# Seven products of quarters for six of eight c and h tiles and for the gates of a gated-convolution decoder step, with a second read of its input

## The chip, the cores and the metric

The kernel runs on one core of one Trainium2 chip. The metric is the device time of one execution in microseconds (us), lower is better. "The time" of a kernel is the median of its runs; the profile comes from one more execution.

## The reference, cut to what matters

The program is one layer of a decoder for 576 tokens (512 of a prompt, 64 of samples) of 1024 channels, all in float32. In this document's names:

```python
xn = rms_norm(h, g_mix)
z = xn @ w_in                         # 1024 x 6144: b, c, hc, v, gate a, gate b
ya = b * conv_w3(c * hc) @ w_out_conv
yb = pool(v) @ w_pool * pool_scale    # trailing means minus the token, by groups
h = h + (sigmoid(a) * ya + sigmoid(bg) * yb) @ w_o
h = h + square(relu(rms_norm(h, g_mlp) @ w_up)) @ w_down
h = h + sigmoid(rms_norm(h, g_ple) @ w_ple_gate) * (p @ w_ple_proj)
y = rms_norm(h, g_final)
```

The last rows of the convolution's and the pooling's inputs are outputs too.

## The kernel before, in words

Channels lie on the partitions, in 8 tiles of 128; the tokens lie in two halves of 288 columns. Every operand is split into a rounded part and the rest (`hi` and `lo`, lines 82 to 94: one cast on ScalarE, one subtraction on VectorE), and every product is three matmuls: hi x hi, hi x lo, lo x hi. A product of one output tile (`product`, line 113) is 8 k x 3 x 2 halves = 48 matmuls of 288 columns. Weights are streamed: `Stream` (line 175) takes a list `order` of parts (128 x 512), loads them on SP's queue into eight raw buffers and splits them into seven pairs of buffers (NF = 7), so that up to six split parts lie ahead of the one in use and loads up to six parts ahead of the splits. A part of a plain tile feeds 24 matmuls.

The mixer comes first. Tile 0 of c, h and b is computed as the input arrives (line 358 on, `psf`). Then, for tiles 1 to 7, a loop computes c, h and b (line 372 on): c is scaled by the squared norm (`r1s`, L375), u = c times h (L381, L384), the three taps are one ScalarE and two VectorE operations (L391, L393), b is scaled (L398), multiplied with the convolution (L400, L403) and split as an operand. Eight gate tiles (L415, L417), eight tiles of `w_oc` (L421), and four groups of pooling with their gates (L432 to L483) follow. At this point the scratch and PSUM pools are closed and others opened (line 489 on), w_o is applied and added to the input, which has stayed in `xall` (L609).

The MLP's first product (w_up) is already done with seven products of quarters for each pair of output tiles q and q+4 (`pairs_of`, line 539). The two output tiles, the two halves of the tokens and the two halves of the 1024 inputs make a 2 x 2 by 2 x 2 block product. `Operand` (line 511) holds, for each of four k, split blocks b11, b22, b21 and four differences of blocks t1 to t4. `Form` (line 152) makes weight blocks a, b, d, two sums made by an accumulating DMA on POOL's queue (s1 = c+d, s0 = c+a, L149) and two made on VectorE (s2, L169; s3, L171). One `quarter` (line 495) is 4 k x 3 = 12 matmuls of 288 columns into one PSUM bank; seven per pair, and VectorE combines them with five operations of 288 columns (L564 to L568, L593, L595), after one ScalarE copy (L544). The first MLP block enters late, with the last k of four quarters moved back. Here the matmuls are kept in program order by hand. Elsewhere a scheduler orders each engine's queue ahead of time, by readiness in its model and by place in the program; on the chip each queue runs in order.

After the MLP come w_ple_proj and w_ple_gate (`psg`), and the final norm.

Of the kernel before, what the change touches and what calls it, by code (L numbers as in the profile page):

```python
# [7 lines left out]
F32 = mybir.dt.float32  # L8
# [4 lines left out]
P = 128  # L13
D = 1024
NJ = D // P
# [27 lines left out]
def tile_hybrid_step(ctx: ExitStack, tc: tile.TileContext, x, pt, vecs, rc, ident, sconv, spool, w_first, w_in,  # L43
# [12 lines left out]
    tmp = scope.enter_context(tc.tile_pool(name="tmpx", bufs=8))  # L56
    psum = scope.enter_context(tc.tile_pool(name="psumx", bufs=4, space=bass.MemoryType.PSUM))
    banks = None

    def matmul(*args, **kw):  # L60

        i = nc.tensor.matmul(*args, **kw)  # L62
        if banks is not None:
            tc.keep_in_program_order(i)
# [158 lines left out]
    for b in range(NFB):  # L223
        pairs = [Pair(w_up[b * NJ + q], w_up[b * NJ + NQ + q]) for q in range(NQ)]
        order += [Form(pairs[0], "a")]
        for q in range(NQ):
            order += [Form(pairs[q], n) for n in ("s2", "s0", "s1", "b")]
            if q + 1 < NQ:
                order += [Form(pairs[q + 1], "a")]
            order += [Form(pairs[q], n) for n in ("d", "s3")]  # L230
        for j in range(NJ):
            order += unit(w_down[b * NJ + j])
# [13 lines left out]
    xall = const.tile([P, NJ, NH, HT], F32, tag="xall", name="xall")  # L246
    xs = [xall[:, j] for j in range(NJ)]
# [44 lines left out]
    sp = tmp.tile([P, NJ, DB, PB], F32, tag="sp", name="sp", bufs=1)  # L292
    nc.sync.dma_start(sp, spool)


    class Rms:
# [48 lines left out]
        def copies(self, r, tag, square=None):  # L345
            out = const.tile(self.shape, F32, tag=tag, name=tag)
# [5 lines left out]
            return out, out2  # L352


    stat = Rms()
    for j in range(NJ):
        stat.add(xs[j], part=j >= NJ - 2)
    ps0 = [psum.tile([P, NH, 512], F32, tag="ps", name="psf") for _ in range(3)]
# [8 lines left out]
    ncp_t = tmp.tile([P, NJ, CW - 1], F32, tag="ncp", name="ncp_t", bufs=1)  # L367
    npp_t = tmp.tile([P, NJ, PB], F32, tag="npp", name="npp_t", bufs=1)


    ya_in = []
    for j in range(NJ):
        ps_c = ps0[0] if j == 0 else product(stream.take(2), xg)
        c = tmp.tile([P, NH, HT], F32, tag="t", name="c")
        nc.vector.tensor_tensor(out=c, in0=halves(ps_c), in1=r1s, op=ALU.mult)  # L375
        ps_h = ps0[1] if j == 0 else product(stream.take(2), xg)
        u = tmp.tile([P, CEXT], F32, tag="ext", bufs=4, name="u")
        us = u[:, CE:].rearrange("p (b t) -> p b t", b=DB)
        nc.gpsimd.memset(u[:, :CW - 1], 0.0)
        nc.gpsimd.tensor_copy(us[:, :, :CW - 1], sc[:, j])  # L380
        nc.vector.tensor_tensor(  # L381
            out=u[:, CW - 1:CE].rearrange("p (h t) -> p h t", h=NH),
            in0=prompt(ps_h), in1=prompt(c), op=ALU.mult)
        nc.vector.tensor_tensor(  # L384
            out=us[:, :, CW - 1:].rearrange("p (h b) t -> p h b t", h=NH),
            in0=sample(ps_h), in1=sample(c), op=ALU.mult)
        nc.gpsimd.tensor_copy(ncp_t[:, j], u[:, CE - (CW - 1):CE])
        nc.gpsimd.tensor_copy(sc[:, j], us[:, :, DS:])
        n = CEXT - (CW - 1)
        cv = tmp.tile([P, CEXT], F32, tag="ext", bufs=4, name="cv")  # L390
        nc.scalar.mul(cv[:, :n], u[:, :n], v(W_CONV, j))  # L391
        for k in range(1, CW):
            nc.vector.scalar_tensor_tensor(  # L393
                out=cv[:, :n], in0=u[:, k:k + n], scalar=v(W_CONV + k, j), in1=cv[:, :n],
                op0=ALU.mult, op1=ALU.add)
        ps_b = ps0[2] if j == 0 else product(stream.take(2), xg)
        bt = tmp.tile([P, NH, HT], F32, tag="t", name="bt")
        nc.vector.tensor_tensor(out=bt, in0=halves(ps_b), in1=r1, op=ALU.mult)  # L398
        ya = tmp.tile([P, NH, HT], F32, tag="t", name="ya")
        nc.vector.tensor_tensor(  # L400
            out=prompt(ya), in0=prompt(bt), in1=cv[:, :SEQ].rearrange("p (h t) -> p h t", h=NH),
            op=ALU.mult)
        nc.vector.tensor_tensor(  # L403
            out=sample(ya), in0=sample(bt),
            in1=cv[:, CE:].rearrange("p (b t) -> p b t", b=DB)[:, :, :DS].rearrange(
                "p (h b) t -> p h b t", h=NH),
            op=ALU.mult)
        ya_in.append(split_act(ya))


    mix = []
    for j in range(NJ):
        ps = product(stream.take(2), xg)
        z = tmp.tile([P, NH, HT], F32, tag="t", name="z")
        nc.vector.tensor_tensor(out=z, in0=halves(ps), in1=r1, op=ALU.mult)  # L415
        g = keep.tile([P, NH, HT], F32, tag="keep", name="ga")
        nc.scalar.activation(g, z, AF.Sigmoid)  # L417
        mix.append(g)
# [66 lines left out]
    for o, t in ((ncp, ncp_t), (ncs, sc), (npp, npp_t), (nps, sp)):  # L485
        nc.sync.dma_start(o, t)
# [3 lines left out]
    tmp = scope.enter_context(tc.tile_pool(name="tmpm", bufs=3))  # L490
    psum = scope.enter_context(tc.tile_pool(name="psumm", bufs=1, space=bass.MemoryType.PSUM))
    banks = scope.enter_context(tc.tile_pool(name="banks", bufs=6, space=bass.MemoryType.PSUM))
    acts2 = scope.enter_context(tc.tile_pool(name="acts2", bufs=6))

    def quarter(o, w, bs, ks, start, stop):
        for k in ks:
            wh, wl = (t[:, k * P:(k + 1) * P] for t in w)
            hi, lo = bs[k]
            for i, (wt, at) in enumerate(((wh, hi), (wh, lo), (wl, hi))):
                matmul(o, wt, at, start=start and k == 0 and i == 0,  # L500
                       stop=stop and k == NQ - 1 and i == 2, skip_group_check=True)

    def two_products(operands, ks):

        two = [(w, [bank() for _ in range(NH)]) for w in (stream.take(2), stream.take(2, live=2))]
        for part in (ks[:-2], ks[-2:]):
            for w, ps in two:
                steps(ps, w, operands, part, first=ks[0], last=ks[-1])
        return [ps for _, ps in two]

    class Operand:

        def __init__(self):
            self.f = {n: [None] * NQ for n in ("b11", "b22", "b21", "t1", "t3", "t2", "t4")}
            self.shared = None

        def two(self, k, src, names):
            parts = split(src, [P, NH, HT], acts2 if k == 0 else acts, "act")
            for i, n in enumerate(names):
                self.f[n][k] = tuple(t[:, i] for t in parts)  # L520

        def add(self, k, g):

            if k % 2 == 0:
                self.shared = tuple(acts.tile([P, NH, HT], F32R, tag="act", name=n) for n in ("hi", "lo"))
            self.two(k, g[:, 1:3], ("b11", "b22"))
            hi, lo = (t[:, k % 2] for t in self.shared)
            nc.scalar.copy(hi, g[:, 3])
            nc.vector.tensor_tensor(out=lo, in0=g[:, 3], in1=as32(hi), op=ALU.subtract)
            self.f["b21"][k] = hi, lo  # L530
            t = tmp.tile([P, 4, HT], F32, tag="g", name="gt", bufs=2)
            nc.vector.tensor_tensor(  # L532
                out=t[:, 0:2], in0=g[:, 0:1].broadcast_to([P, 2, HT]), in1=g[:, 1:3], op=ALU.subtract)
            nc.vector.tensor_tensor(out=t[:, 2], in0=g[:, 2], in1=t[:, 0], op=ALU.subtract)  # L534
            nc.vector.tensor_tensor(out=t[:, 3], in0=g[:, 3], in1=t[:, 2], op=ALU.subtract)
            self.two(k, t[:, 0:2], ("t1", "t3"))
            self.two(k, t[:, 2:4], ("t2", "t4"))

    def pairs_of(n, op, corner, finish, late=False, between=None):


        def copied(pa):
            g = tmp.tile([P, 4, HT], F32, tag="g", name="g", bufs=2)
            nc.scalar.copy(g[:, 1], pa)  # L544
            return g

        def begin(w):
            pa = bank()
            quarter(pa, w, op.f["b11"], range(NQ), True, True)
            return pa, copied(pa)  # L550
# [264 lines left out]
```

## Time and profile before

| | us |
|---|---|
| median of 3 runs | 907.16 (905.72 to 907.32) |
| the profiled execution, its own time | 907.29 |
| its span, first to last instruction | 905.5 |
| TensorE busy | 890.5 |
| VectorE busy | 520.6 |
| ScalarE busy | 374.4 |
| GpSimd busy | 111.2 |

PE is TensorE's matmuls, PEld its weight loads, DVE VectorE, ACT ScalarE, POOL GpSimd, SP the queue that issues most DMAs. A letter q behind an engine means its instruction queue. L89 is line 89 of the kernel. The profiled execution's time is 1.8 us longer than its span.

### The profile page before, as it was taken

Reading aid. Unit: us, or ns where it says so; the run is one execution under the profiler, and the core shown is the slowest. Engines: PE = TensorE matmul, PEld = TensorE weight load, DVE = VectorE, ACT = ScalarE, POOL = GpSimd, SP = SyncE. Lnnn points to the kernel's source line nnn. Section 1 sums busy time; section 2 is a strip of 40 time slices with the busy share of each in tenths; the row PEclk is TensorE's granted clock in tenths of the full one; section 3 lists DMA queues with packets and bytes.
Section 4 is the critical chain, followed back from the end, with each engine's and each line's share of the span. In section 5 each row is a group of like instructions: output and inputs, shape, how many; then the busy total and the mean of one; then the engine's idle time right before and its main releaser. Section 6 shows DMA issues by size and latency. Waiting matters only on the chain.

```text
span 905.5 us, 16619 instructions
## 1 busy us (share of the span) xinstructions
PE 890.5 (98%) x6674; PEld 887.7 (98%) x6674; DVE 520.6 (57%) x880; ACT 374.4 (41%) x642; POOL 111.2 (12%) x148
## 2 busy tenths in 40 slices
PE   9999999999999999999999999999999999999995
PEld 8999999999999999999999999999999999999995
DVE  7554544433335767857884337633773467687455
ACT  8332222322112333344675337622673157546432
POOL 3000000000002210112110100010100110021354
PEclk9999999999999999999999999999999999999998
DMA  7422222222222222334453545444544444332002
GB/s 256 156 82 84 82 83 82 85 83 82 82 83 85 81 82 86 112 83 95 118 160 99 140 106 140 128 112 110 137 133 105 111 125 134 97 96 93 24 10 96
DMA packets 52654, 93.66 MB, mean 103 GB/s; under 512 B 6241, under 2 KB 9953, under 8 KB 52577
## 3 DMA queue, kind: packets, MB, share of 16 engines
q1 hardware_dynamic: 47824, 84.18, 29.5%
q0 software_dynamic: 4608, 8.39, 5.9%
q8 instruction: 52, 0.85, 0.4%
q14 instruction: 26, 0.20, 0.1%
q10 hardware_dynamic: 144, 0.03, 0.0%
HBM read 89.60 MB, written 2.99 MB: 102 GB/s over the span
## 4 chain that ended last, share of the span: by engine, by line
PE 93%; DVE 3%; ACT 1%; issue 1%; DMA 1%; SPq 0%; DVEq 0%; ACTq 0%
PE b L62 46%; PE ps L62 39%; PE psg L62 6%; PE psf L62 2%; DVE lo L89 1%; PE psn L322 1%; PE psn L340 1%; DMA raw<-w_up 1%; DMA xall<-x 1%; DVE xall L609 0%; ACT hi L88 0%; DVE gt L534 0%; DVE gt L532 0%; DVE xall L697 0%; ACT sq L307 0%
## 5 line engine op out<-in xcount | busy, mean ns | idle before, releaser
L88 ACT CAST hi<-raw 128x512 fp32r<-128x512 f32 x290 | 178.5, 621 | 384.4 <-PE ps L62 205.6
L89 DVE TENSOR_TENSOR lo<-raw,hi 128x512 fp32r<-128x512 f32 x290 | 204.4, 709 | 145.8 <-ACT hi L88 140.9
L62 PE MATMUL b<-hi 128*128 128x288 f32 x1120 | 276.4, 296 | 2.7 <-ACT hi L88 1.3
L62 PE MATMUL b<-lo,hi 128*128 128x288 f32 x1120 | 275.9, 295 | 0.1
L62 PE MATMUL b<-hi,lo 128*128 128x288 f32 x1120 | 275.9, 295 | 0.0
L62 PEld LDWEIGHTS b<-hi 128*128 128x128 f32 x1120 | 192.3, 188 | 3.7 <-ACT hi L88 1.7
L62 PEld LDWEIGHTS b<-lo,hi 128*128 128x128 f32 x1120 | 192.3, 188 | 0.3 <-DVE lo L89 0.3
L62 PEld LDWEIGHTS b<-hi,lo 128*128 128x128 f32 x1120 | 192.3, 188 | 0.0
L62 PE MATMUL ps<-lo,hi 128*128 128x288 f32 x880 | 188.5, 296 | 0.0
L62 PE MATMUL ps<-hi 128*128 128x288 f32 x880 | 188.5, 296 | 0.0
L62 PE MATMUL ps<-hi,lo 128*128 128x288 f32 x880 | 188.3, 296 | 0.0
L62 PEld LDWEIGHTS ps<-hi 128*128 128x128 f32 x880 | 141.9, 189 | 0.0
L62 PEld LDWEIGHTS ps<-lo,hi 128*128 128x128 f32 x880 | 141.9, 189 | 0.0
L62 PEld LDWEIGHTS ps<-hi,lo 128*128 128x128 f32 x880 | 141.9, 189 | 0.0
L149 POOL DMA_DIRECT2D raw<-w_up x32 | 27.9, 872 | 326.4 <-DMA raw<-w_up 186.1
L313 POOL TENSOR_TENSOR sq<-sq 128x576 f32<-128x576 f32 (+2 forms) x32 | 41.1, 1284 | 113.1 <-ACT sq L307 63.8
L62 PE MATMUL psg<-hi 128*128 128x320 f32 (+1 forms) x128 | 38.1, 298 | 0.7 <-ACT r L347 0.7
L62 PE MATMUL psg<-lo,hi 128*128 128x320 f32 (+1 forms) x128 | 37.9, 296 | 0.0
L62 PE MATMUL psg<-hi,lo 128*128 128x320 f32 (+1 forms) x128 | 37.9, 296 | 0.0
L89 DVE TENSOR_TENSOR lo<-s,hi 128x512 fp32r<-128x512 f32 x32 | 22.0, 691 | 15.8 <-ACT hi L88 15.1
L89 DVE TENSOR_TENSOR lo<-g,hi 128x576 fp32r<-128x576 f32 x32 | 26.4, 834 | 6.6 <-ACT hi L88 6.6
L307 ACT ACTIVATE sq<-xall 128x576 f32<-128x576 f32 (+2 forms) x39 | 22.5, 585 | 18.1 <-DVE xall L726 18.1
(124 smaller groups left out, 704.0 us busy)
## 6 DMA issues: line engine op xcount, KB each, us to landing
raw<-w_in SPq DMA_DIRECT2D x90, 256.0 KB, 2.7
raw<-w_up SPq DMA_DIRECT2D x80, 256.0 KB, 2.9
raw<-w_down SPq DMA_DIRECT2D x64, 256.0 KB, 2.9
raw<-w_up POOLq DMA_DIRECT2D x32, 256.0 KB, 4.3
raw<-w_oc SPq DMA_DIRECT2D x16, 256.0 KB, 2.7
raw<-w_o SPq DMA_DIRECT2D x16, 256.0 KB, 2.7
raw<-w_pg SPq DMA_DIRECT2D x16, 256.0 KB, 2.8
xall<-x SPq DMA_DIRECT2D x7, 288.0 KB, 5.3
```

Source lines behind the costliest of these rows:

```text
L62: i = nc.tensor.matmul(*args, **kw)
L88: nc.scalar.copy(hi, src)
L89: nc.vector.tensor_tensor(out=lo, in0=src, in1=as32(hi), op=ALU.subtract)
L149: nc.gpsimd.dma_start(raw, y, accum_op=ALU.add)
L307: i = nc.scalar.activation(sq, t, AF.Square)
L313: nc.gpsimd.tensor_tensor(out=self.parts[0], in0=self.parts[0], in1=sq, op=ALU.add)
L322: nc.tensor.matmul(sums[:, i:i + 1], a[:, h, c:c + m], ones32[:, 0:1], start=k == 0, stop=k == len(self.parts) - 1)
L340: nc.tensor.matmul(self.ps[:, h, c:c + m], self.y[:, i:i + 1].broadcast_to([m, P]), idt[:m, :m], start=True, stop=True)
```

## The change

Tiles 1 to 3 and 5 to 7 of c and of h, and all eight gate tiles, are computed in pairs (q, q+4) by the seven products of quarters; tiles 0 and 4 of c and h, and all tiles of b, stay plain. In a block of one q the pair of c comes first, then the pair of h with b of tile q in between (`filler`), then b of tile q+4. The operand is the scaled input `xg`, whose split tiles serve as b11, b22 and b21 as they are; only the differences are made, in the iterations of tiles 0 and 4, in part in ten buffers of their own. The matmuls of these parts are kept in program order. The convolution becomes a class with parts by half. The mixer's scratch has four buffers of a tile instead of eight; pools are opened so that a new tile waits for the old tiles under it alone (`reuse_waits="tile"`), and one set of pools more is used (gates and pooling are now in different ones). The input lies in the eight `keep` buffers, which the gates take over, and is loaded a second time into `xall` when the pooling ends. The pooling state is loaded, and the convolution state stored, between the gates and `w_oc`. Helpers moved up unchanged are left out here.

```diff
-    tmp = scope.enter_context(tc.tile_pool(name="tmpx", bufs=8))
-    psum = scope.enter_context(tc.tile_pool(name="psumx", bufs=4, space=bass.MemoryType.PSUM))
+    def pool(name, bufs, **kw):
+        return scope.enter_context(tc.tile_pool(name=name, bufs=bufs, reuse_waits="tile", **kw))
+    tmp, acts2 = pool("tmpx", 4), pool("acts1", 10)
+    psum = pool("psumx", 1, space=bass.MemoryType.PSUM)
+    banks = pool("banksx", 6, space=bass.MemoryType.PSUM)
...
-    for j in range(1, NJ):
-        order += unit(w_in[NJ + j]) + unit(w_in[2 * NJ + j]) + unit(w_in[j])
-    for j in range(NJ):
-        order += unit(w_in[4 * NJ + j])
+    order += unit(w_in[NJ + NQ]) + unit(w_in[2 * NJ + NQ]) + unit(w_in[NQ])
...
+    for q in range(1, NQ):
+        order += forms([Pair(w_in[i * NJ + q], w_in[i * NJ + NQ + q]) for i in (1, 2)],
+                       unit(w_in[q]), unit(w_in[NQ + q]))
+    order += forms([Pair(w_in[4 * NJ + q], w_in[4 * NJ + NQ + q]) for q in range(NQ)])
...
-    xall = const.tile([P, NJ, NH, HT], F32, tag="xall", name="xall")
-    xs = [xall[:, j] for j in range(NJ)]
+    xs = [keep.tile([P, NH, HT], F32, tag="keep", name="xin") for _ in range(NJ)]
...
+    ya_in = [None] * NJ
+    for j in (0, NQ):
...
+        conv.gate(ps0[2] if j == 0 else product(stream.take(2), xg))
+        for k in range(j // 2, j // 2 + 2):
+            g = tmp.tile([P, 4, HT], F32, tag="g", name="gx", bufs=2)
+            for i in range(2):
+                nc.scalar.mul(g[:, 2 * i:2 * i + 2], xs[k + i * NQ], v(G_MIX, k + i * NQ))
+            xo.differences(k, g)
+    pinned = True
+    for q in range(1, NQ):
+        def corner(i, g, c11):
+            if i == 0:
+                conv.lo = tmp.tile([P, NH, HT], F32, tag="t", name="c")
+                nc.vector.tensor_tensor(out=conv.lo[:, 1], in0=c11, in1=r1s[:, 1], op=ALU.mult)
+            else:
+                conv.now.half(1, c11, conv.lo[:, 1])
+        def finish(i, g):
+            if i == 0:
+                nc.vector.tensor_tensor(out=conv.lo[:, 0], in0=g[:, 0], in1=r1s[:, 0], op=ALU.mult)
+                conv.hi = tmp.tile([P, NH, HT], F32, tag="t", name="c")
+                nc.vector.tensor_tensor(out=conv.hi, in0=g[:, 2:4], in1=r1s, op=ALU.mult)
+                conv.now = Conv(q)
+            else:
+                conv.now.half(0, g[:, 0], conv.lo[:, 0])
+                conv.now.convolve()
+                conv.then = Conv(q + NQ)
+                conv.then.whole(g[:, 2:4], conv.hi)
+                conv.now.gate(conv.ps)
+                conv.then.convolve()
+        def filler():
+            conv.ps = product(stream.take(2), xg)
+        pairs_of(2, xo, corner, finish, filler=filler)
+        conv.then.gate(product(stream.take(2), xg))
...
+    pairs_of(NQ, xo, corner, finish)
+    pinned = False
+    for o, t in ((ncp, ncp_t), (ncs, sc)):
+        nc.sync.dma_start(o, t)
+    scope.close()
+    tmp = pool("tmpp", 8)
+    psum = pool("psump", 4, space=bass.MemoryType.PSUM)
+    sp = tmp.tile([P, NJ, DB, PB], F32, tag="sp", name="sp", bufs=1)
+    nc.sync.dma_start(sp, spool)
...
     scope.close()
+    xpool = ctx.enter_context(tc.tile_pool(name="xpool", bufs=1, reuse_waits="tile"))
+    xall = xpool.tile([P, NJ, NH, HT], F32, tag="xall", name="xall")
+    xs = [xall[:, j] for j in range(NJ)]
+    for j in halved:
+        nc.sync.dma_start(xs[j], x[:, j])
```

## Rows read from the trace of the kernel before

**Rows 1.** The head of the page and its part 1, busy time of TensorE.
```profile
span 905.5 us, 16619 instructions
...
PE 890.5 (98%) x6674; PEld 887.7 (98%) x6674; DVE 520.6 (57%) x880; ACT 374.4 (41%) x642; POOL 111.2 (12%) x148
```

**Rows 2.** Chain that ended last, in order of time: start, length, what.
```profile
32.53 350.41 PE ps L62 x2628
...
477.33 354.39 PE b L62 x2664
```

**Rows 3.** Waits of TensorE: total us, times, longest.
```profile
PE b L62 <- ACT hi L88: 1.3, 2, 0.7
...
PE b L62 <- DVE t L480: 1.0, 1, 1.0
...
PE psg L62 <- ACT r L347: 0.7, 1, 0.7
...
PE b L62 <- ACT g L544: 0.5, 1, 0.5
```

**Rows 4.** Busy time by stretch: stretch, length, each engine's busy us, clock, DMA, GB/s.
```profile
20.00:30.00 10.00, 10.00 (x81) 10.00 (x80) 6.48 (x15) 3.23 (x5) 0.00 (x0) 0.83 0.81 260
30.00:40.00 10.00, 10.00 (x77) 10.00 (x77) 7.64 (x13) 4.54 (x7) 0.56 (x4) 1.00 0.24 81
40.00:50.00 10.00, 10.00 (x77) 10.00 (x77) 4.71 (x8) 2.66 (x4) 1.02 (x4) 1.00 0.24 81
360.00:370.00 10.00, 10.00 (x77) 10.00 (x77) 8.43 (x17) 2.47 (x4) 2.95 (x6) 1.00 0.26 81
430.00:440.00 10.00, 10.00 (x78) 10.00 (x77) 8.90 (x16) 6.12 (x11) 2.25 (x2) 1.00 0.49 132
440.00:450.00 10.00, 9.44 (x68) 8.81 (x67) 9.20 (x19) 6.61 (x14) 1.44 (x2) 1.00 0.43 107
541.60:585.90 44.30, 44.30 (x336) 44.30 (x335) 33.25 (x59) 31.58 (x54) 1.73 (x2) 1.00 0.51 141
...
32.50:165.00 132.50, 132.50 (x996) 132.50 (x995) 67.63 (x109) 37.03 (x57) 7.80 (x32) 1.00 0.26 82
```

**Rows 5.** Groups of VectorE by line and shape: busy us, mean ns; idle before.
```profile
L89 DVE TENSOR_TENSOR lo<-raw,hi 128x512 fp32r<-128x512 f32 x290 | 204.4, 709 | 145.8 <-ACT hi L88 140.9 <-DMA raw<-w_in 3.0
...
L393 DVE SCALAR_TENSOR_TENSOR cv<-u,vec,cv 128x592 f32<-128x592 f32 x16 | 13.3, 834 | 2.9 <-ACT cv L391 2.6
L171 DVE SCALAR_TENSOR_TENSOR s<-s,raw 128x512 f32<-128x512 f32 x16 | 12.4, 777 | 0.2
...
L593 DVE TENSOR_TENSOR g<-b,u 128x288 f32<-128x288 f32 x16 | 7.3, 456 | 5.3 <-PE b L62 5.3
...
L89 DVE TENSOR_TENSOR lo<-ya,hi 128x576 fp32r<-128x576 f32 x8 | 6.1, 759 | 5.3 <-ACT hi L88 5.2
...
L400 DVE TENSOR_TENSOR ya<-bt,cv 128x512 f32<-128x512 f32 x8 | 5.5, 684 | 0.0
...
L398 DVE TENSOR_TENSOR bt<-ps,r 128x576 f32<-128x576 f32 x7 | 5.3, 757 | 14.5 <-PE ps L62 14.5
...
L403 DVE TENSOR_TENSOR ya<-bt,cv 128x64 f32<-128x64 f32 x8 | 1.7, 216 | 0.0
```

**Rows 6.** DMA issues: queue, count, size of one, median us to landing.
```profile
raw<-w_up POOLq DMA_DIRECT2D x32, 256.0 KB, 4.3
...
xall<-x SPq DMA_DIRECT2D x7, 288.0 KB, 5.3
```

**Rows 7.** Order of time in the MLP, POOL and VectorE: start, us, idle before.
```profile
456.55 2.47 DVE L89 TENSOR_TENSOR lo<-g,hi 128x576 fp32r<-128x576 f32 x1
456.62 3.67 POOL L313 TENSOR_TENSOR sq<-sq 128x576 f32<-128x576 f32 x2
...
553.12 0.86 POOL L149 DMA_DIRECT2D raw<-w_up  x1 [4.72 <-DVE s L169]
553.53 0.69 DVE L89 TENSOR_TENSOR lo<-s,hi 128x512 fp32r<-128x512 f32 x1 [0.37 <-ACT hi L88]
```

More of the change, by code (lines that the diff above doesn't have):

```diff
@@ L223, in tile_hybrid_step @@
     for b in range(NFB):
[L224 to L230, printed above, removed]
+        order += forms([Pair(w_up[b * NJ + q], w_up[b * NJ + NQ + q]) for q in range(NQ)])
         for j in range(NJ):
@@ L352, in copies, with quarter, two_products @@
             return out, out2
+    def quarter(o, w, bs, ks, start, stop):
+        for k in ks:
+            wh, wl = (t[:, k * P:(k + 1) * P] for t in w)
+            hi, lo = bs[k]
+            for i, (wt, at) in enumerate(((wh, hi), (wh, lo), (wl, hi))):
+                matmul(o, wt, at, start=start and k == 0 and i == 0,
+                       stop=stop and k == NQ - 1 and i == 2, skip_group_check=True)
+    def two_products(operands, ks):
+        two = [(w, [bank() for _ in range(NH)]) for w in (stream.take(2), stream.take(2, live=2))]
+        for part in (ks[:-2], ks[-2:]):
+            for w, ps in two:
+                steps(ps, w, operands, part, first=ks[0], last=ks[-1])
+        return [ps for _, ps in two]
@@ new lines, in tile_hybrid_step, with __init__, two, add @@
+    class Operand:
+        def __init__(self, spare):
+            self.spare = spare
+            self.f = {n: [None] * NQ for n in ("b11", "b22", "b21", "t1", "t3", "t2", "t4")}
+            self.shared = None
+        def two(self, k, src, names):
+            self.spare -= 2
+            parts = split(src, [P, NH, HT], acts2 if self.spare >= 0 else acts, "act")
+            for i, n in enumerate(names):
+                self.f[n][k] = tuple(t[:, i] for t in parts)
+        def add(self, k, g):
+            if k % 2 == 0:
+                self.shared = tuple(acts.tile([P, NH, HT], F32R, tag="act", name=n) for n in ("hi", "lo"))
+            self.two(k, g[:, 1:3], ("b11", "b22"))
+            hi, lo = (t[:, k % 2] for t in self.shared)
+            nc.scalar.copy(hi, g[:, 3])
+            nc.vector.tensor_tensor(out=lo, in0=g[:, 3], in1=as32(hi), op=ALU.subtract)
+            self.f["b21"][k] = hi, lo
+            self.differences(k, g)
+        def plain(self, k, a, b):
+            for n, t, h in (("b11", a, 1), ("b22", b, 0), ("b21", b, 1)):
+                self.f[n][k] = tuple(p[:, h] for p in t)
+        def differences(self, k, g):
+            t = tmp.tile([P, 4, HT], F32, tag="g", name="gt", bufs=2)
+            nc.vector.tensor_tensor(
+                out=t[:, 0:2], in0=g[:, 0:1].broadcast_to([P, 2, HT]), in1=g[:, 1:3], op=ALU.subtract)
+            nc.vector.tensor_tensor(out=t[:, 2], in0=g[:, 2], in1=t[:, 0], op=ALU.subtract)
+            nc.vector.tensor_tensor(out=t[:, 3], in0=g[:, 3], in1=t[:, 2], op=ALU.subtract)
+            self.two(k, t[:, 0:2], ("t1", "t3"))
+            self.two(k, t[:, 2:4], ("t2", "t4"))
@@ L357, in tile_hybrid_step @@
         stat.add(xs[j], part=j >= NJ - 2)
-    ps0 = [psum.tile([P, NH, 512], F32, tag="ps", name="psf") for _ in range(3)]
+    ps0 = [[bank() for _ in range(NH)] for _ in range(3)]
     for k in range(NJ):
@@ L388, in tile_hybrid_step @@
[L388 to L397, printed above, removed]
@@ L408, in tile_hybrid_step @@
[L408 to L418, printed above, removed]
+        conv = Conv(j)
+        for h in range(NH):
+            conv.half(h, ps_h[h], c[:, h])
+        conv.convolve()
@@ L483, in tile_hybrid_step @@
             merged.append(split_act(t))
-    for o, t in ((ncp, ncp_t), (ncs, sc), (npp, npp_t), (nps, sp)):
+    for o, t in ((npp, npp_t), (nps, sp)):
         nc.sync.dma_start(o, t)
     scope.close()
[L490 to L537, printed above, removed]
```

234 lines of the change are left out of this document (145 added, 89 removed).

## The prediction

> **What bounds the kernel now.** I read the head of the page first: TensorE is busy 890.5 of 905.5 us [rows 1]. The reader should not take the 98% alone as proof, because a busy mark says nothing about waiting inside it. So the second view is the chain that ended last, in order of time [rows 2]. There one stretch of 350.41 us is nothing but products of the mixer, back to back, and a later one of 354.39 us nothing but products of the MLP. The first stretch holds 55 products of 48 matmuls, 2640 in all, so a matmul of 288 columns is issued every 350.41 / 2640 = 0.1327 us. The third view, the waits of TensorE, lists what stopped it after the start: four entries, 3.5 us together [rows 3]. Hence time here is the number of matmuls times 0.1327 us plus very little, and a matmul removed from the mixer is worth its full pitch as long as VectorE, ScalarE and the loads keep the operands ready. The fourth view, busy time by stretch, says how much room those have [rows 4].
>
> **What is removed.** Two output tiles take 2 x 48 = 96 matmuls as plain products; as seven products of quarters they take 7 x 12 = 84. There are three pairs of c, three of h and four of gates: 10 pairs, 120 matmuls, 120 x 0.1327 = 15.9 us. The MLP already works in this form, and its stretch from 541.6 to 585.9 shows 336 matmuls, which is 4 x 84, in 44.30 us without a gap [rows 4], so the pitch of a quarter is the same 0.132 us and the form does what it says.
>
> **What is added in a block of c, h and b** (one q: two pairs and two plain products, 264 matmuls, 35.0 us of TensorE). VectorE, by the means of its groups [rows 5]: 18 weight splits x 0.709 = 12.8; four sums of weights x 0.777 = 3.1; ten combinations of quarters x 0.456 = 4.6; scaling c 0.46 + 0.46 + 0.76 = 1.7; the products c times h 2 x (0.46 + 0.22) + 0.68 + 0.22 = 2.2; four convolution steps x 0.834 = 3.3; two gatings, each 2 x 0.46 + 0.68 + 0.22 + 0.76 = 2.6, 5.1. Sum 32.8 us. Means overlap when operations follow each other: the same sum for an MLP pair is 7 x 0.709 + 2 x 0.777 + 5 x 0.456 + 2 x 0.759 = 10.3 us, 16 operations; the stretch of four pairs holds 59 of VectorE's operations, 38.0 us by that mean, in 33.25 us of busy time [rows 4], a factor of 0.875. So a block needs about 28.7 of its 35.0 us, 82%. Before, 132.5 us of this stage had 67.63 us of VectorE, 51%. The gate pairs cost what an MLP pair costs, 75%. TensorE ran without a gap in slices with VectorE at 8.43 and 8.90 of 10 us, but lost 0.56 us in one at 9.20 [rows 4]. I therefore cost a block at 0.5 us of stall, 1.5 us for three. From below: 0 (a gain is excluded, TensorE's work is already counted). From above: after the second b22 quarter, h's product, the convolutions of both tiles and the first gating come in one burst of about 9 us with the second gating, against 6.4 us of plain product beside them; all of the surplus exposed is 2.8 us a block, 8.4 us. I stay near the low end because the row with 8.90 is nearest to the 82%. The work is covered by weight splits kept six ahead; if that cover is gone, each late VectorE operation costs its own length.
>
> **The entry to the first pair.** The t-operands of all four k must be split before the t2 quarter ends. Per k that is one subtraction of 576 columns, two of 288 and two splits of 576: 0.757 + 2 x 0.456 + 2 x 0.759 = 3.2 us, 12.8 for four, 11.2 with the factor. They need only the input, so they can fill idle time: VectorE left 3.52, 2.36 and 5.29 us free in the three slices from 20 to 50 us [rows 4], 11.2 us together. TensorE reaches the last k of t2 at about 32.5 + 144 x 0.1327 + 21 x 0.1327 = 54.4 us. It just fits, and a schedule is never packed perfectly, so I take 1.5 us. From below 0; from above, with k = 2 and 3 standing behind the gating of tile 4 in program order, 2.6 + 2 x 3.2 = 9.0 us less 2.8 us of work that TensorE still has (the b11 quarter and the first nine of t2), 6.2 us. The nearest row is the MLP's own entry, whose waits are 1.3 and 0.5 us [rows 3].
>
> **Moved and re-read.** The input goes to buffers that the gates later take over, and is loaded again, eight loads on SP's queue, when the pooling stage closes. The first of them waits for the last scratch tile: after the last pooled product four operations of the 0.76 to 0.83 us class [rows 5], some 3 us; landing took 5.3 us where seven such loads ran beside weights [rows 6]. TensorE meanwhile has 96 matmuls, 12.7 us, before the first sum needs it: margin 4 us, cost 0. If that cover goes, sums are late, then PSUM banks, then TensorE; a load held up by two weight steps of 24 matmuls is 6.4 us later, and with what then follows I bound the stall at 6 us. Weights behind these loads on SP's queue are up to twelve parts ahead, over 30 us. State loads moved later cost 0 for the same reason.
>
> **Pools released tile by tile.** The first matmul on w_o waited 1.0 us for the last reader of the old pool's PSUM [rows 3]; with other banks free this goes: -1.0. What is late next is the last merged tile, covered by the first six k of two products. The same for the w_ple_gate stage, 0.7 us, I leave at zero, since its first bank may be the one still read; bounds 0 and -0.7.
>
> **Loads.** A pair loads seven parts instead of four, two of them with an accumulating transfer on POOL's queue. The MLP's stretch carries this at 141 GB/s with TensorE full [rows 4]: cost 0, covered by the loads ahead.
>
> POOL's accumulating issues stand beside VectorE's splits: at 553.12 one of 0.86 us ran while VectorE took its usual 0.69, but two POOL additions of 3.67 us together stretched a 576-column split to 2.47 [rows 7]. The Trainium skill (GPSIMD Engine Reference, Key points) says GpSimd shares its SBUF interfaces with VectorE and contends with operations that have two SBUF inputs. By that rule the four new issues of a block would also slow VectorE, by up to 4 x 0.86 = 3.4 us, to 32.1 of 35.0 us, and the time would go half of the way to the first rival, about 899; by the trace it stays at the sum below. The trace agrees for POOL's arithmetic and not for its issues, and the blocks hold only small POOL copies.
>
> **Sum.** The profiled execution took 907.29 us, 0.13 over the median 907.16. 907.29 - 15.9 - 1.0 + 1.5 + 1.5 = 893.4 us.
>
> **Rivals.** *VectorE becomes the bound in the blocks.* For it: 82% with bursts, an engine that works in order, four buffers of scratch instead of eight. Against: gapless slices at 84 and 89%. At full price 8.4 + 6.2 in place of 3.0: 905.0; half of the way, about 899. *The second reading of the input comes late*: 6 us, 899.4. For it: one tile holds all eight, so the first load waits for every scratch tile under it. *Slower:* the accumulating transfers of the next block stand on POOL's queue behind the copies of the new state, which wait for h's product at the block's end. From there a part needs issue 0.86 [rows 7], landing 4.3 [rows 6], sum 0.78 and two casts of at most 0.71 [rows 5], 7.3 us; exposed in three blocks 21.9 us in place of 1.5, and the time is 907.29 - 15.9 - 1.0 + 1.5 + 21.9 = 913.8. It decides when TensorE has less than 7.3 us of split weights left at that point, and the whole turns slower from 5.1 us a block. Against it: loads are issued up to twelve parts ahead, and in the MLP POOL waited 4.72 us for a buffer before its issue at 553.12 [rows 7] without a gap on TensorE [rows 4].
>
> **How the numbers follow.** Forecast 66% (889.7 to 897); VectorE-bound 18%; late input 8%; POOL's order 4%; 4% for a tail of several small stalls that eats the gain. A difference of 0.2%, 1.8 us, is about what a measurement of this kernel can tell from none. Faster than 905.3 are the first three nearly whole: 0.93; same 0.03; slower 0.04. The range goes from all stalls at zero and both pool waits gone, 907.29 - 15.9 - 1.7 = 889.7, up to 901, two thirds of the way into VectorE's full price.
>
> **What would show it.** TensorE's instructions 120 fewer and busy near 875 us; pitch in the mixer unchanged at 0.133; TensorE's waits near 50 us on differences (lo of gt) of 0 to 3 us; VectorE near 80% in the c and h blocks; the wait for t at the start of w_o gone; no wait for the input's second load. It is wrong if the clock row leaves 1.00 in the mixer, if waits on weight splits or on banks recur in every block, or if sums on w_o wait for a transfer.

## The result, and the profile after

| | before | after |
|---|---|---|
| median (lowest to highest), us | 907.24 of 4 runs (905.72 to 907.54) | 897.68 of 4 runs (895.12 to 897.96) |
| the profiled execution, us | 907.29 | 897.59 |

The ratio of after to before is 0.9892, with an interval of 0.987 to 0.9913: faster by 1.1%, some 9.6 us. The forecast was 893.4 us in a range of 889.7 to 901.0. Direction and range held, but the time is 4.2 us above the forecast, and the sections below show that several terms of the sum were wrong in ways that partly cancelled. One execution of experiment 6 (3022.89 us) and one of the kernel before beside experiments 5 to 8 (3080.58 us) stand far outside all others and are in no median or ratio below.

The head of the page after and the busy time of the engines, to be set beside [rows 1]:

```profile
span 895.8 us, 16709 instructions
...
PE 878.8 (98%) x6554; PEld 875.5 (98%) x6554; DVE 581.2 (65%) x1027; ACT 405.0 (45%) x702; POOL 131.1 (15%) x168
```

TensorE has 6554 matmuls instead of 6674: the 120 are gone. Yet its busy time fell by 11.7 us only, against 16.0 for 120 matmuls at the pitch of before (the chain's row of [rows 2] counts 2628 matmuls in 350.41 us, 0.1333 us each). So some of the remaining matmuls must have become longer. The pitch is the time from one matmul to the next. The prediction has it as 0.1327 us, for it divides the 350.41 us by all 2640 matmuls of the 55 products; the last twelve of them come after this piece of the chain.

The chain that ended last, in order of time (start, length, what), answers to [rows 2]:

```profile
34.09 20.49 PE b L67 x155
54.60 0.63 ACT hi L93
55.25 2.08 DVE lo L94 x3
57.36 0.77 DVE gt L409
...
59.84 0.77 DVE lo L94
60.65 148.76 PE b L67 x1106
209.41 164.79 PE ps L67 x1236
...
467.57 354.39 PE b L67 x2664
```

One unbroken chain of products has become two, with six microseconds of VectorE and ScalarE between them: the entry to the first pair. After it, 1106 matmuls run without a stop, then the plain products of `w_oc` and the pooling as before. The MLP's long stretch is 354.39 us in both. TensorE's waits say the same, beside [rows 3] (total us, times, longest):

```profile
PE b L67 <- ACT hi L93: 3.6, 3, 1.9
...
PE b L67 <- DVE lo L94: 1.1, 3, 0.5
PE b L67 <- DVE t L691: 1.0, 1, 1.0
...
PE psg L67 <- ACT r L354: 0.7, 1, 0.7
```

The first row was 1.3 us before. The wait for t at the start of w_o and the wait for r before w_ple_gate are unchanged.

**An account by marks.** Four marks stand in every trace: M, the first plain product after tile 0; O, the first product of `w_oc`; S, the start of the MLP's long stretch; and the end. Each length is a difference of starts in the chain of waits. Before, O lies inside the piece of 350.41 us; it is put 164.79 us ahead of that piece's end, the length of the same matmuls after.

| us | before | after | difference |
|---|---|---|---|
| start to M | 32.53 | 34.09 | +1.56 |
| M to O: c, h, b and gates | 185.62 | 175.32 | -10.30 |
| O to S: `w_oc`, pooling, w_o, entry of the MLP | 259.18 | 258.16 | -1.02 |
| S to the end, and the time outside the span | 429.96 | 430.02 | +0.06 |
| the profiled execution | 907.29 | 897.59 | -9.70 |

All but 1 us of the gain lies from M to O. There it is 5.6 us short of the 15.9 of the count, where the forecast had allowed 3.0 for stalls.

**Inside the entry.** Busy time by stretch (columns as in [rows 4]) around it, and two later ones:

```profile
50.00:55.00 5.00, 5.00 (x40) 5.00 (x40) 4.11 (x9) 1.75 (x4) 0.00 (x0) 1.00 0.31 108
55.00:60.00 5.00, 1.57 (x8) 0.88 (x6) 4.73 (x10) 2.98 (x6) 0.00 (x0) 0.82 0.15 52
60.00:65.00 5.00, 4.82 (x19) 4.50 (x20) 2.93 (x6) 1.34 (x3) 0.00 (x0) 0.50 0.00 0
...
90.00:100.00 10.00, 10.00 (x78) 10.00 (x77) 9.78 (x20) 5.31 (x9) 2.42 (x7) 1.00 0.36 109
...
67.00:209.40 142.40, 142.40 (x1078) 142.40 (x1077) 114.04 (x220) 64.15 (x110) 21.63 (x39) 1.00 0.54 143
```

From 55 to 60 us the row shows 8 matmuls. From 60 to 65 TensorE is busy again, but with only 19 where the row of 50 to 55 us has 40: the granted clock is 0.50, which is 1.2 of 2.4 GHz. That answers the question of the busy time in part; the first stage adds to it, whose clock from 20 to 30 us is 0.71 here against 0.83 before (experiment 7). The later rows show a VectorE at 9.78 of 10 us without a gap on TensorE, and at 80% over the 142 us that follow the entry.

VectorE's instructions there, in order of time (start, us, line, what, idle before with its releaser):

```profile
53.00 0.82 DVE L542 TENSOR_TENSOR bt<-b,r 128x288 f32<-128x288 f32 x2 [0.89 <-PE b L67]
...
55.90 0.76 DVE L94 TENSOR_TENSOR lo<-bt,hi 128x576 fp32r<-128x576 f32 x1
56.57 0.75 DVE L94 TENSOR_TENSOR lo<-gt,hi 128x576 fp32r<-128x576 f32 x1
57.36 0.76 DVE L409 TENSOR_TENSOR gt<-gx 128x576 f32<-128x576 f32 x1
```

And TensorE's at the same place:

```profile
56.49 0.40 PE L67 MATMUL b<-hi 128*128 128x288 f32 x1 [1.00 <-ACT hi L93]
57.38 0.40 PE L67 MATMUL b<-lo,hi 128*128 128x288 f32 x1 [0.49 <-DVE lo L94]
...
59.86 0.61 PE L67 MATMUL b<-hi 128*128 128x288 f32 x1 [1.95 <-ACT hi L93]
60.65 0.61 PE L67 MATMUL b<-lo,hi 128*128 128x288 f32 x1 [0.18 <-DVE lo L94]
```

VectorE's queue has the gating of tile 4 (53.00, it waits for TensorE's b product) and the split of its result (55.90) ahead of the last split of k = 2 (56.57), and all of k = 3 (from 57.36) behind that (k is one of the four tiles of the halved input, t2 the first quarter that needs differences). TensorE stands before k = 2 of t2 at 55.5 and before k = 3 from 57.9. Its four idle gaps are 1.00, 0.49, 1.95 and 0.18 us, 3.6 together. By the matmuls issued the loss is larger: the 40 from 52.93 to 65.11 took 12.2 us instead of 5.3, a loss of 6.9. Of it 3.6 us are idle, 1.8 are the 17 matmuls from 61 to 65 us at 0.24 us each instead of 0.133, and the rest lies in the few matmuls between and right behind the gaps.

### The profile page after: what moved, and what is told of

Read it like the earlier page. It is cut to its first block, busy times and chain, and to the rows that moved or that the text cites. A ratio compares the mean times of both kernels' runs of the same rounds, so it can differ in the third digit from the quotient of the medians.

```text
span 895.8 us, 16709 instructions
## 1 busy us (share of the span) xinstructions
PE 878.8 (98%) x6554; PEld 875.5 (98%) x6554; DVE 581.2 (65%) x1027; ACT 405.0 (45%) x702; POOL 131.1 (15%) x168
## 4 chain that ended last, share of the span: by engine, by line
PE 94%; DVE 3%; DMA 1%; ACT 1%; issue 1%; SPq 0%; DVEq 0%
PE b L67 68%; PE ps L67 18%; PE psg L67 6%; DVE lo L94 1%; PE psn L329 1%; PE psn L347 1%; DMA raw<-w_up 1%; DMA xin<-x 0%; ACT hi L93 0%; DVE xall L808 0%; DVE t L691 0%; DVE gt L409 0%; ACT hi L96 0%; DVE gt L412 0%; DVE gt L411 0%
## 5 line engine op out<-in xcount | busy, mean ns | idle before, releaser
L67 PE MATMUL b<-hi 128*128 128x288 f32 x1592 | 403.1, 298 | 5.2 <-ACT hi L93 3.6
L67 PE MATMUL b<-lo,hi 128*128 128x288 f32 x1592 | 402.1, 297 | 0.7 <-DVE lo L94 0.7
L67 PE MATMUL b<-hi,lo 128*128 128x288 f32 x1592 | 402.1, 297 | 0.4 <-DVE lo L94 0.4
L67 PEld LDWEIGHTS b<-hi 128*128 128x128 f32 x1592 | 278.0, 190 | 6.8 <-ACT hi L93 4.3
L67 PEld LDWEIGHTS b<-lo,hi 128*128 128x128 f32 x1592 | 278.1, 190 | 1.3 <-DVE lo L94 1.2
L67 PEld LDWEIGHTS b<-hi,lo 128*128 128x128 f32 x1592 | 277.7, 190 | 0.7 <-DVE lo L94 0.7
L67 PE MATMUL ps<-hi 128*128 128x288 f32 x416 | 89.2, 296 | 0.0
L67 PE MATMUL ps<-hi,lo 128*128 128x288 f32 x416 | 89.1, 296 | 0.0
L67 PE MATMUL ps<-lo,hi 128*128 128x288 f32 x416 | 89.1, 296 | 0.0
L67 PEld LDWEIGHTS ps<-hi,lo 128*128 128x128 f32 x416 | 67.0, 189 | 0.0
```

## Experiments

The changed kernel is the base of each, and each diff is against it. Beside the times stands M to O of the profiled execution, since start to M differs from one execution to the next. The marks are differences of the chain's starts throughout. The kernel before, run beside the experiments, had medians of 907.53 us (the first four), 908.40 (the next four) and 907.77 (the last three).

### 1. The last k moved back at the first pair

The MLP's own entry computes k = 0 to 2 of four quarters before the last k of any. Here the first pair of c does so too.

```diff
-        pairs_of(2, xo, corner, finish, filler=filler)
+        pairs_of(2, xo, corner, finish, q == 1, filler=filler)
```

> The first pair of c enters late: the last of four k moves to the end of its first quarters, VectorE's order is unchanged. Theory (the differences of k = 2 and 3 reach TensorE late, and the gap then costs half speed as well): TensorE still waits some 1.5 to 2 us for k = 2, but no longer for k = 3, and its clock stays at 1.00; about 5 of the 6.9 us lost at the entry come back, 892 to 893.5 us. Rival (the splits of the weights are late at the entry, not the differences): no more than 1 us comes back, 896.5 to 898.

Measured: median 892.12 us (891.57 to 895.98), ratio 0.9826 [0.9805, 0.9848]. The profiled execution was the slowest of the four, 895.98; its M to O is 172.94 us, 2.4 below after. TensorE still waits there, for k = 2, and the clock falls less:

```profile
50.00:60.00 10.00, 8.12 (x53) 7.66 (x53) 8.19 (x15) 3.69 (x6) 0.00 (x0) 0.91 0.23 79
60.00:70.00 10.00, 9.92 (x68) 9.53 (x67) 7.59 (x15) 4.65 (x10) 0.86 (x1) 0.92 0.22 64
```

The wait for k = 3 is gone, as expected, but the clock did not stay at 1.00: two gaps, of 1.40 and 0.49 us, are followed by some 3 us of matmuls at 0.24 us each. More work ahead of the late operands helps, but doesn't remove the wait, because k = 2 was late too. VectorE's order did change in one place: the split of a weight sum, 0.7 us, that stood ahead of the split of tile 4 stands behind the differences here. The median is inside the theory's 892 to 893.5 us and 5.6 below that of the changed kernel, of which M to O shows 2.4; the rest is not attributed.

### 2. All four splits in the iteration of tile 0

The differences of k = 2 and 3 need only the input. The edit places them before tile 4 instead of behind its gating.

```diff
-        for k in range(j // 2, j // 2 + 2):
+        for k in range(NQ) if j == 0 else ():
```

> All four k of differences stand behind tile 0 in the program, none behind tile 4. Theory (they are late because of their place, behind the gating of tile 4 on VectorE's queue): the differences end before 52 us, no wait at the entry, no fall of the clock, 890 to 892 us. Rival (VectorE has no time for them before the entry, whatever the order): what is moved behind them is late in their place, TensorE waits for weight splits or PSUM banks near 45 to 60 us, 895 us or more.

Measured: median 889.61 us (888.28 to 890.26), ratio 0.9799 [0.9779, 0.9819], just below the theory's 890 to 892; again on another chip, beside the changed kernel itself (label g2_early):

> Two splits up front alone. By the theory of the entry (6.9 us lost there by TensorE): 6 to 8 us below g3_after on the same chip. Rival, that the entry costs only its idle time of 3.6 us: 3.5 to 4.5 us below g3_after.

890.08 us (889.48 to 891.64) against 896.42 (894.86 to 898.27) for the changed kernel, 6.3 us less, inside the 6 to 8 of the first theory and outside the rival's 3.5 to 4.5. The chain, and the stretches at the old place of the entry, from the first of the two:

```profile
32.58 168.91 PE b L67 x1272
201.49 164.79 PE ps L67 x1236
```

```profile
50.00:60.00 10.00, 10.00 (x78) 10.00 (x77) 9.68 (x19) 4.59 (x9) 1.96 (x4) 1.00 0.35 112
60.00:70.00 10.00, 10.00 (x78) 10.00 (x77) 6.64 (x13) 4.47 (x9) 1.72 (x2) 1.00 0.74 200
```

M to O is one piece again, 168.91 us: 16.71 below before and 6.41 below after. The last split of a difference ends at 49.2 us, against 60.6 in the changed kernel. The gaps are gone and so is the fall of the clock; no work was taken out, the same work only stands earlier in the queues of VectorE and ScalarE. That settles the cause of the entry's cost. The first block alone, from its first matmul to that of the next block, takes 34.94 us here and 41.81 in the changed kernel, 6.9 more; M to O shows 0.46 less of it, because tile 4's 144 matmuls ahead of the block took 18.84 us there and 19.30 here. In a second execution of the changed kernel (label g3_after) the four gaps come again, 0.99, 0.49, 1.95 and 0.18 us, and the block takes 42.07 us.

### 3. b of tile 1 computed ahead of the first pair

A rival cure: 48 plain matmuls, 6.4 us, ahead of the pair give VectorE time, at the old place in its queue.

```diff
+    order += unit(w_in[1])
...
-                       unit(w_in[q]), unit(w_in[NQ + q]))
+                       unit(w_in[q]) if q > 1 else (), unit(w_in[NQ + q]))
...
-        pairs_of(2, xo, corner, finish, filler=filler)
+        if q == 1:
+            filler()
+        pairs_of(2, xo, corner, finish, filler=filler if q > 1 else None)
```

> The plain product of b for tile 1 (48 matmuls, 6.4 us of TensorE) is moved ahead of the first pair instead of into its second half. Theory and rival on VectorE's time both give VectorE 6.4 us more before the entry, against 3.6 us of waiting: no gap, no fall of the clock, 890 to 892 us. If banks or the rhythm of the weights set the entry, it stays at 896 or more.

Measured: median 890.64 us (888.13 to 891.86), ratio 0.9808 [0.9784, 0.9833]; M to O 170.61. The entry has no wait, but at 80 us there is a new one, with an accumulating transfer in its chain. The wait, the piece of the chain, and VectorE's instructions there:

```profile
PE b L67 <- DVE g L446: 1.3, 1, 1.3
```

```profile
72.39 6.51 DMA raw<-w_in
```

```profile
78.92 0.69 DVE L174 TENSOR_TENSOR s<-raw 128x512 f32<-128x512 f32 x1 [3.61 <-DMA raw<-w_in]
79.53 0.45 DVE L446 TENSOR_TENSOR g<-b,g 128x288 f32<-128x288 f32 x1
```

VectorE stood idle for 3.61 us at a weight sum that waited for the transfer, the combination `g` (L446) stood behind that sum, and TensorE waited 1.32 us for `g`. It is the entry's mechanism at another place: an instruction held up by one that waits ahead of it in the queue. The plain product that was moved had lain in the second pair of this block; that it was the cover there is the likely reading, and no run tests it alone. The granted clock stays at 1.00 from 80 to 85 us, behind this single gap.

### 4. The gates alone in pairs

All tiles of c and h plain, as before; the operand split in the loop of tiles as in the changed kernel. It takes out 48 of the 120 matmuls and separates the c and h blocks from the gates.

```diff
-    order += unit(w_in[NJ + NQ]) + unit(w_in[2 * NJ + NQ]) + unit(w_in[NQ])
+    for j in range(1, NJ):
+        order += unit(w_in[NJ + j]) + unit(w_in[2 * NJ + j]) + unit(w_in[j])
...
-    for j in (0, NQ):
+    for j in range(NJ):
...
-        for k in range(j // 2, j // 2 + 2):
+        for k in range(j // 2, j // 2 + 2) if j in (0, NQ) else ():
```

(The loop over the blocks of c, h and b and its parts in `order` go out with it.)

> The gates alone in pairs; c and h of all tiles plain; everything else as in the changed kernel. 48 matmuls fewer than the kernel before, 6.4 us. The differences are needed only some 130 us later. Theory (the loss of the changed kernel is its entry and nothing in the pairs themselves): the full 6.4 us come, 900 to 901.5 us, with no wait of TensorE between 40 and 360 us. Rival (pairs lose time in each block, by VectorE): part of it stays away, 902.5 or more, with waits in the gates' stretch.

Measured: median 900.45 us (899.05 to 902.96), ratio 0.9923 [0.9899, 0.9948]; no wait in the mixer, M to O 179.26 us in one piece of 1344 matmuls, 0.1334 each. The gate pairs give their full count: 48 x 0.1333 = 6.4 us of M to O. The step from here to experiment 2 adds the c and h pairs with a clean entry: 72 matmuls, 9.6 us by count, and 10.35 of M to O measured. So the blocks of c and h cost nothing beside their matmuls. The time is inside the theory's 900 to 901.5 us.

### 5. Useless matmuls in the wait

To price the clock apart from the idle time, 30 matmuls into a spare bank (4.0 us) are put between k = 1 and k = 2 of the first t2 quarter. VectorE's queue stays as it is in the changed kernel.

```diff
-                    quarter(o, stream.take()[0], op.f[name], range(NQ), True, True)
+                    w = stream.take()[0]
+                    if idle and i == 0 and x == 0:
+                        quarter(o, w, op.f[name], range(2), True, True)
+                        spare = psum.tile([P, NH, 512], F32, tag="ps", name="spare")
+                        for _ in range(idle):
+                            matmul(spare[:, 0, :HT], w[0][:, :P], op.f[name][0][0], start=True, stop=True)
+                        quarter(o, w, op.f[name], range(2, NQ), False, True)
+                    else:
+                        quarter(o, w, op.f[name], range(NQ), True, True)
...
-        pairs_of(2, xo, corner, finish, filler=filler)
+        pairs_of(2, xo, corner, finish, filler=filler, idle=30 if q == 1 else 0)
```

> The changed kernel with 30 matmuls more, 4.0 us, that compute nothing needed, between the second and the third k of the first t2 quarter, where TensorE stood idle. Theory (the entry cost 3.6 us of waiting and about as much again because the granted clock then fell to half): the clock stays at 1.00 between 50 and 70 us, the entry costs the 4.0 us of added work and at most 0.6 us of waiting in place of 6.9 us, so the added work makes the kernel faster, 894.5 to 896. Rival (waiting alone is the loss, the clock costs little): 4.0 us of work in place of 3.6 us of waiting, 897.5 to 899.

Measured: median 896.13 us (894.98 to 896.75), ratio 0.986 [0.9844, 0.9877]; M to O 173.84, 1.5 us below after although 4.0 us of useless work are in it. The useless matmuls in order of time, and the stretches that follow:

```profile
54.23 4.16 PE L67 MATMUL spare<-hi 128*128 128x288 f32 x30
```

```profile
55.00:60.00 5.00, 4.61 (x33) 4.19 (x32) 4.32 (x7) 1.99 (x5) 0.00 (x0) 1.00 0.05 20
60.00:65.00 5.00, 5.00 (x40) 5.00 (x38) 4.02 (x8) 2.06 (x4) 0.00 (x0) 1.00 0.13 43
```

The clock stays at 1.00 and one wait of 0.4 us is left. With the clock held, the entry costs 173.84 - 168.91 = 4.9 us instead of 6.4: the operands are late by up to 4.0 + 0.4 us, and some 1.5 us of the loss is the clock alone. By the first block it is 1.9 us: 39.87 us here, 41.81 in the changed kernel. The times alone would not settle it: 896.13 us is just above the theory's 894.5 to 896 and below the rival's 897.5 to 899, but the interval of its ratio overlaps that of the changed kernel.

### 6. The accumulators' pool opened first at w_o

The forecast's 1.0 us for the wait for t at w_o had not come. Two pools are opened there; by the theory their order says which of the old banks each gets. The edit stands on experiment 2.

```diff
-    psum = pool("psumm", 1, space=bass.MemoryType.PSUM)
     banks = pool("banks", 6, space=bass.MemoryType.PSUM)
+    psum = pool("psumm", 1, space=bass.MemoryType.PSUM)
```

> Early differences as in e2_early, and at w_o the six single banks are opened ahead of the pool of two banks, so that they lie on other banks than before. Theory (w_o's first matmul waits 1.0 us because its bank is still the one that the last pooled product is read from): the wait for t goes, and so does the 0.7 us wait of the w_ple_gate stage, 888 to 889 us against e2_early's 889.6. Rival (the wait is on the whole pool or on VectorE's queue, not on a bank): the same 1.0 us wait, the same time.

Measured: three runs of 885.81 to 888.51 us, ratio 0.9766 [0.9744, 0.9788]. Beside experiment 2 and the changed kernel on one chip (label g1_best):

> Two splits up front and the pool of accumulators opened ahead of the other one at the MLP's entry. If both gains add: 1.0 to 2.0 us below g2_early on the same chip (1.0 for the missing wait for t and 0.7 for the missing wait for r), 8 to 10 us below g3_after. Rival, that the gain of the banks was only the first stage's clock in one execution: within 0.5 us of g2_early.

887.02 us (885.19 to 887.57), 3.1 below the 890.08 of experiment 2, every run below every run of it, and 9.4 below the changed kernel. That is more than the two waits' 1.7 us and the 1.0 to 2.0 expected. The profiled pair differs by 6.3 us: 3.0 from start to M, where the first stage has its own clock, and 3.3 behind M, 1.6 of them from S to the end, where the wait for r was. So the rival's half microsecond is out, and the rest of the excess is not attributed. In neither profile is there a wait for t or r. Of the first of these runs, the chain and, below it, the stretch at the start of w_o:

```profile
30.72 168.45 PE b L67 x1272
199.17 166.38 PE ps L67 x1248
```

```profile
370.00:380.00 10.00, 10.00 (x77) 10.00 (x76) 3.95 (x8) 3.63 (x6) 0.86 (x1) 1.00 0.83 285
```

The same stretch of the changed kernel, where the wait for t was:

```profile
370.00:380.00 10.00, 9.01 (x68) 8.77 (x67) 6.84 (x10) 3.17 (x5) 0.00 (x0) 1.00 0.34 101
```

The piece of plain products ends at 199.17 + 166.38 = 365.55 us and the next one, on w_o, starts right there; in the changed kernel three operations on t stand between. So the wait goes with the order of opening. That the pool of six, opened first, gets banks whose last reader is done is the theory's reading; the trace doesn't show which banks they are. This is the best version of the study: ratio to before 0.9767 [0.9747, 0.9786].

### 7. The norm's narrow matmuls spread out

Start to M was 30.6 to 34.2 us in these traces, and its difference is the clock from 20 to 30 us. A theory was that the block of narrow matmuls of the norm (36 of line 329 in one piece) lets it fall. On top of experiment 2 they go between tile 0's products in three groups.

```diff
-        if k == 5:
-            stat.tokens()
+            if k == 5:
+                stat.tokens(group=u)
```

(The method `tokens`, which then does one group at a time, is left out.)

> Early differences as in e2_early, and the 36 narrow matmuls that sum the squares of the norm stand in three groups between the products of tile 0 instead of in one. Theory (the granted clock falls after this block of narrow matmuls, in some executions for longer than in others, and that is most of the spread of a few us between executions): the clock is 1.00 in the slices from 20 to 40 us, the time 887.5 to 888.5, the executions within 1 us. Rival (the clock falls from something else at this place): the same clock of 0.83 or less, 889 to 890 us.

Measured: median 888.67 us (887.62 to 892.0), ratio 0.9786 [0.9762, 0.9811]; the profiled execution, the slowest, has the lowest clock of all in this stretch, here beside the one of experiment 6, whose narrow matmuls stand in one block:

```profile
20.00:30.00 10.00, 10.00 (x67) 10.00 (x66) 7.96 (x19) 6.37 (x11) 1.90 (x2) 0.67 0.71 163
```

```profile
20.00:30.00 10.00, 10.00 (x93) 10.00 (x92) 9.08 (x21) 7.65 (x13) 1.90 (x2) 1.00 0.71 182
```

The theory fell. What decides the clock there stays open: it was 0.83 before, 0.71 and 1.00 in two profiled executions of the changed kernel, 0.83 and 0.69 in two of experiment 2.

### 8. The input read twice over

To see the margin of the re-read, its eight loads are issued twice, on top of experiment 2.

```diff
-    for j in halved:
-        nc.sync.dma_start(xs[j], x[:, j])
+    for _ in range(2):
+        for j in halved:
+            nc.sync.dma_start(xs[j], x[:, j])
```

> Early differences as in e2_early, and the input is loaded into its buffer twice, one set of eight loads after the other (16 loads, 2.4 MB more). Theory (the second reading of the input lies in the shadow of w_o's first two products with some 7 us to spare): about 5 us later and still hidden, no wait of TensorE at w_o beyond the one for t, within 0.5 us of e2_early's 889.6. Rival (the reading is at its limit): sums on w_o wait, then banks, then TensorE, 892 us or more.

Measured: median 891.79 us (890.6 to 892.97), ratio 0.9817 [0.9796, 0.9839]. The sixteen issues last from 369.7 to 379.8 us. The sums, by line (least, median and most ns, first and last time):

```profile
L720 DVE TENSOR_TENSOR xall<-b,xall x16: 441/448/457, 381.2 to 421.9; 128x288 f32<-128x288 f32 x16
```

The same line of experiment 2:

```profile
L719 DVE TENSOR_TENSOR xall<-b,xall x16: 443/448/458, 380.0 to 419.7; 128x288 f32<-128x288 f32 x16
```

w_o starts at 368.73 here and at 368.86 there, so the first sum comes 12.5 us after it instead of 11.1, 1.3 late, with twice the loads ahead of it. TensorE shows no wait for it beside the 1.0 for t. The median is 2.2 us above experiment 2, but on another chip, and O to S (259.58 against 257.33) was 259.56 in experiment 5, which loads once. The median lies between the theory's 0.5 us around 889.6 and the rival's 892 or more. What the 2.2 us are is not settled.

### The changed kernel again

It ran unedited beside the last two as their reference.

> The changed kernel itself, unedited, on the same chip: 896 to 898 us, 9 to 11 us below the kernel before by both theories; it is the reference of the two others.

Measured: 896.42 us (894.86 to 898.27), ratio to before 0.9878 [0.9857, 0.9899], 11.4 us below it. The result repeats on a second chip.

## Why the prediction was right, and where it was not

The forecast was 893.4 us, and the profiled execution took 897.59. The range held although the entry alone cost 4.9 us more than forecast, because the blocks cost 1.5 less, the count gave 0.8 more and O to S another 1.0, which has no known cause; in part that is luck. The terms against the traces:

| term | forecast, us | measured, us | by |
|---|---|---|---|
| 120 matmuls fewer | -15.9 | -16.71 | M to O of experiment 2 against before |
| stalls in the c and h blocks | +1.5 | 0 | no wait from 65 us to O; experiments 2 and 4 |
| entry to the first pair | +1.5 | +6.41 | M to O of after against experiment 2 |
| wait for t at w_o | -1.0 | 0 | the wait's row; gone in experiment 6 |
| start to M | 0 | +1.56 | the marks; clock of the first stage |
| O to S | 0 | -1.02 | the marks; not attributed |

The last two differ about as much between executions of equal code (start to M 32.58 and 34.01, O to S 257.33 and 258.15 in the two of experiment 2).

**The count: right.** At the plain products' pitch of 0.1333 us, not the 0.1327 of the prediction, the 120 are 16.0 us. The 0.7 us beyond are a slightly shorter pitch of what remains. In experiment 2 the three blocks, the gates and `w_oc` start at 51.88, 86.82, 121.76, 156.70 and 201.33 us: 0.1323 us a matmul in the blocks and 0.1328 in the gates, which over their 1128 matmuls is about 1 us. Why it is shorter is open. The form gives its 12 matmuls a pair, for gates and for c and h alike (experiments 4 and 2).

**The blocks: right in the load, too dear in the price.** A block was to need VectorE for 28.7 of 35.0 us. The second and the third, which have no entry in them, show 29.1 and 28.0 (by the starts of their first matmuls, at 94.75, 129.69 and 164.63 us):

```profile
94.76:129.69 34.93, 34.93 (x267) 34.93 (x266) 29.07 (x58) 14.91 (x25) 6.20 (x14) 1.00 0.53 137
129.69:164.65 34.96, 34.96 (x267) 34.96 (x266) 27.98 (x55) 13.94 (x24) 6.97 (x12) 1.00 0.54 140
```

TensorE loses nothing in them, nor in a slice at 9.78 of 10. The row at 9.20 with 0.56 us lost [rows 4] was no measure of the price: a VectorE that was busy for nearly all of a slice didn't stop TensorE here. The rival of a VectorE bound fell with it. By the prediction's estimate, the rule on shared interfaces that it takes from the Trainium skill (GPSIMD Engine Reference, Key points) would have cost up to 3.4 us a block for the accumulating issues. The runs side with the trace of before: the weight splits, 128 x 512, have a mean of 707 ns in this kernel against 709 in [rows 5], and the 37 splits (of parts and of sums) that ran beside an accumulating issue took 686 ns on average, none over 694:

```profile
L94 DVE TENSOR_TENSOR lo<-raw,hi 128x512 fp32r<-128x512 f32 x300 | 210.6, 707 | 112.0 <-ACT hi L93 108.9
```

**The entry: the step that failed.** The prediction counted the work that VectorE had to do (11.2 us) against the idle time that it had (11.2 us), and took 1.5 us. Its upper bound, 6.2 us, was built on the right mechanism, k = 2 and 3 standing behind the gating of tile 4 in program order. That mechanism happened: a queue in fixed order can't use idle time with work that stands behind a wait. And the bound was still too low in kind: it priced idle time alone, of which 3.6 us came, while a TensorE that came back at half its clock lost 1.5 to 1.9 us more. The prediction had named a clock row below 1.00 in the mixer as what would make it wrong, and gave it no price.

**The wait at w_o: wrong.** "With other banks free this goes" took free banks for granted to be the ones handed out. The order in which the two pools are opened decides whether the wait comes, as experiment 6 shows. The same edit also removed the wait of 0.7 us before w_ple_gate, which the prediction had left at zero with the right doubt.

**The second reading of the input: right.** The issues and the first sum, by line:

```profile
L705 SPq DMA_DIRECT2D xall<-x x8: 423/430/1417, 377.8 to 382.1; - x8
...
L719 DVE TENSOR_TENSOR xall<-b,xall x16: 440/447/458, 388.2 to 428.5; 128x288 f32<-128x288 f32 x16
```

The loads landed 4.8 us after issue by their median, so the first was there at about 382.6, some 5.6 us ahead of the first sum, where a margin of 4 had been worked out. No wait of TensorE names it.

**The slower rival: its place is real, its price was not paid.** In the first block VectorE and POOL, in order of time:

```profile
84.46 0.69 DVE L174 TENSOR_TENSOR s<-raw 128x512 f32<-128x512 f32 x1 [4.50 <-DMA raw<-w_in]
```

```profile
79.06 0.86 POOL L154 DMA_DIRECT2D raw<-w_in  x1 [5.18 <-DVE lo L94]
85.55 0.68 POOL L528 COPY ncp_t<-u 128x2 f32<-128x2 f32 x1 [5.63 <-DVE u L511]
86.17 0.86 POOL L154 DMA_DIRECT2D raw<-w_in  x1
```

An issue stands at 86.17 behind a state copy that waited 5.63 us for `u`, as the rival has it. But `u` was late because VectorE stood idle for 4.50 us at a sum ahead of it, whose transfer had been issued at 79.06, before the copy. TensorE shows no gap there. Where a plain product was moved away, in experiment 3, a wait of 1.3 us behind such a sum did come.

## What to carry to other kernels

Total idle time of an engine says nothing about whether late work fits: look at which instruction it stands behind in the queue, and place work that depends only on old data ahead of the first wait for new data. Price a gap on TensorE by what the matmuls after it take too, not only by its idle time; here 3.6 us of idle time came to a loss of 6.4 or more. When pools of accumulators are closed and reopened, check which bank the first new product may get; here the order of opening alone made a wait of 1.0 us.

## What was not expected of the hardware

The granted clock fell to 0.50 with no single gap of TensorE over 1.95 us: four gaps of 3.6 us together, with few matmuls between them. Two gaps of 1.40 and 0.49 us (experiment 1) were followed by matmuls at half speed too, a single one of 1.32 us (experiment 3) was not. 30 useless matmuls of 4.0 us in their place kept it at 1.00, and the time to O was 1.5 us shorter with them.

In the first stage the clock from 20 to 30 us ranged from 0.67 to 1.00 over the traces, with the same code as well, which moves the time by some 3 us; spreading the narrow matmuls didn't explain it, and the cause is open.
